# An encoder layer in one core: first-half tiles by way of DRAM, late residuals by single tiles, differences on another engine

## The chip, the cores and the metric

One core of one Trainium2 chip runs one transformer encoder layer as one program. The metric is the device time of one execution in microseconds (us). A core has TensorE (PE, matmul), VectorE (DVE), ScalarE (ACT), GpSimd (POOL) and SyncE (SP), each with its own instruction stream that runs in order. SP issues nearly all DMAs; POOL issues those that add to what lies at their destination.

## The reference

With S = 2048 tokens, D = 1024, FFN_HIDDEN = 2816, float32, and one layer, only the attention mixer is used:

```python
def rmsnorm(x, g):
    return x * lax.rsqrt(jnp.mean(x * x, axis=-1, keepdims=True) + EPS) * g

def swiglu(h, w_in, w_out):
    a, b = jnp.split(h @ w_in, 2, axis=-1)
    return (jax.nn.silu(a) * b) @ w_out

mod = silu(c) @ ada_w + ada_b
sh1, sc1, g1, sh2, sc2, g2 = split(mod, 6)
h = rmsnorm(x, mix_norm_pre) * (1 + sc1) + sh1
y = windowed_gqa_sink(h, w_qkv, w_o, sink, rel_bias)
x = x + g1 * rmsnorm(y, mix_norm_post)
h = rmsnorm(x, ffn_norm_pre) * (1 + sc2) + sh2
y = swiglu(h, w_in, w_out)
x = x + g2 * rmsnorm(y, ffn_norm_post)
```

## The kernel before

The work is kept transposed: a tile is 128 features by 512 tokens (`CH`). The tokens form four chunks c = 0 to 3, two to a half (`hf` = 0 and 1). The stages follow each other: Q, K, V and their statistics; attention with the output projections filled in (to about 820 us of the profile); the hidden products of the feed-forward (820 to 1690), half by half, each in blocks t = 0 to 21; its output products (1690 to 2125), half by half in four parts of the hidden tiles (`PARTS`); and the end of the second half. Every float32 product is made of three products of a high and a low part. `split` makes these parts: a cast on ACT (L158) and a subtraction on DVE (L159); `three` (L153 to L155) issues the matmuls.

Both feed-forward products use a scheme with seven products of half-size blocks in place of eight. `Block.__init__` loads two raw weight slabs from a pool of two buffers (`raw`, L749 and L750, names wiri and wiro), forms four sums on DVE (L754 to L758) and splits seven operands. `Block.step` runs one of the seven products into one of six PSUM buffers. `Hidden.take` combines the results: additions on DVE that read PSUM (L801 to L817), and then Silu on ACT and a product of the two halves on POOL (L827). The activations also need sums of blocks: `differences` (L526 to L533) forms four of them from a pair of hidden tiles, `give_pair` stores them to `g_d` (L782), and the output stage reads them as hb11o, ht2o and so on (L736).

The first half's residual and norm after attention are done before the hidden stage. Those of chunks 2 and 3 are done beside the hidden blocks of the first half, by the generator `late_residuals`, of which the table `LATE` says how many steps follow each block: y is read back (ly), multiplied by its norm on POOL (L863), x is added by an accumulating DMA of POOL's (L864), the result is stored (L857), squared on ACT (L859) and the squares are added on POOL (L861); then the second norm gives h2 (lh, L505), and for chunk 3 the differences. `late_ada` follows it with the last adaLN products on DVE (L901).

`Outs.take` copies the first part's seven products to z tiles (ACT, L969), a ring of 31 buffers, and adds later parts on DVE (L972); the combinations of L976 run on DVE or POOL. A finished tile is `ys[c, n]`. `square` squares it on ACT (L990) and adds it to zacc (L991). `ends` then forms the norm with `rstd_out`, and `finish` scales each tile on DVE (L1000), adds the attention's residual x1 by an accumulating DMA of POOL's (L1001) and stores it to the output by SP (L1002). For the first half this runs beside the second half's first products, a step for each turn of `interleaved`. `rstd_of` takes the mean by a matmul with ones, then Ln, Exp and Square on ACT and one Newton step on DVE (L144, L145); for that the gains are scaled by -0.5 once.

A scheduler orders each engine's instructions after the program is written. It keeps dependences and buffers, and goes by a simulated time, so a small change of the source moves many instructions.

## Time and profile before

| what | value |
|---|---|
| median of 3 runs | 2178.55 us (2174.4 to 2181.18) |
| the profiled execution | 2181.28 us, its span 2179.5 us, mean granted PE clock 0.982 |
| busy of the span | PE 2053.1 us (94%), DVE 1606.6 (74%), ACT 1069.2 (49%), POOL 870.4 (40%) |
| DMA | 392.69 MB, 180 GB/s over the span |

Busy times are of the span. A window's row gives the busy time of each engine in a stretch; "idle" is what is left of it. A wait's row names the waiting instruction, the one that released it, total time, count and longest. L12 is line 12 of the kernel before.

### The profile page before, as it was taken

Reading aid. Unit: us, or ns where it says so; the run is one execution under the profiler, and the core shown is the slowest. Engines: PE = TensorE matmul, PEld = TensorE weight load, DVE = VectorE, ACT = ScalarE, POOL = GpSimd, SP = SyncE. Lnnn points to the kernel's source line nnn. Section 1 sums busy time; section 2 is a strip of 40 time slices with the busy share of each in tenths; the row PEclk is TensorE's granted clock in tenths of the full one; section 3 lists DMA queues with packets and bytes.
Section 4 is the critical chain, followed back from the end, with each engine's and each line's share of the span. In section 5 each row is a group of like instructions: output and inputs, shape, how many; then the busy total and the mean of one; then the engine's idle time right before and its main releaser. Section 6 shows DMA issues by size and latency. Waiting matters only on the chain. (4 is left out here: it accounts for less than half of the span.)

```text
span 2179.5 us, 29140 instructions
## 1 busy us (share of the span) xinstructions
PE 2053.1 (94%) x9464; PEld 1676.2 (77%) x9464; DVE 1606.6 (74%) x2793; ACT 1069.2 (49%) x2108; POOL 870.4 (40%) x792
## 2 busy tenths in 40 slices
PE   6898999999989979999999999999999899997997
PEld 4786777778867758878878778888888688785886
DVE  7657667665675668878787788777664889997886
ACT  4536666577687745435334243333332554465422
POOL 3403343357679625475375624323212100232043
PEclk9999999999999989999999999999999999999998
DMA  8877655576667595375365663223222545349436
GB/s 283 259 253 235 188 168 185 160 276 221 228 207 265 170 352 186 122 213 174 134 178 178 236 221 135 107 83 112 99 87 83 182 140 179 99 148 268 159 97 136
DMA packets 202821, 392.69 MB, mean 180 GB/s; under 512 B 20347, under 2 KB 68524, under 8 KB 197548
## 3 DMA queue, kind: packets, MB, share of 16 engines
q1 hardware_dynamic: 194028, 378.76, 51.6%
q0 software_dynamic: 8064, 11.54, 3.3%
q8 instruction: 75, 1.23, 0.2%
q14 instruction: 78, 0.64, 0.1%
q10 hardware_dynamic: 576, 0.52, 0.1%
HBM read 266.98 MB, written 123.76 MB: 179 GB/s over the span
## 5 line engine op out<-in xcount | busy, mean ns | idle before, releaser
L442 DVE CUSTOM_DVE_ANT_0 pr<-s,bias,nsink 128x384 f32<-128x384 f32 (+1 forms) x256 | 149.0, 597 | 104.9 <-PE s L437 92.6
L153 PE MATMUL pc_i<-ht,ws_i 128*128 128x512 f32 x528 | 206.3, 391 | 4.0 <-DVE u_i L801 3.3
L155 PE MATMUL pc_i<-ht,ws_i 128*128 128x512 f32 x528 | 205.7, 390 | 0.0
L154 PE MATMUL pc_i<-ht,ws_i 128*128 128x512 f32 x528 | 205.5, 389 | 0.0
L827 POOL TENSOR_TENSOR p_i<-p_i,u_i 128x512 f32<-128x512 f32 x44 | 75.3, 1713 | 317.7 <-ACT wa_i L158 150.1
L444 ACT ACTIVATE pr<-pr,nm 128x385 f32<-128x385 f32 (+1 forms) x256 | 154.0, 605 | 70.8 <-DVE nm L442 65.7
L450 POOL TENSOR_SCALAR pr<-pr,rs 128x384 f32<-128x384 f32 (+1 forms) x256 | 147.2, 600 | 91.5 <-DVE rs L448 91.1
L976 POOL TENSOR_TENSOR z<-z,z 128x512 f32<-128x512 f32 x32 | 53.8, 1698 | 298.0 <-DVE z L972 267.6
L437 PE MATMUL s<-k,q 128*128 128x384 f32 (+1 forms) x512 | 136.8, 361 | 16.7 <-DVE nm L442 9.9
L159 DVE TENSOR_TENSOR wa_i<-wiri,wa_i 128x512 fp32r<-128x512 f32 x126 | 115.7, 918 | 48.6 <-ACT wa_i L158 48.2
L153 PE MATMUL pc_i<-hb,wa_i 128*128 128x512 f32 x352 | 140.1, 398 | 9.2 <-DVE u_i L801 6.9
L159 DVE TENSOR_TENSOR plo<-t,phi 128x512 fp32r<-128x512 f32 x184 | 121.8, 685 | 26.1 <-ACT phi L158 25.0
L155 PE MATMUL pc_i<-hb,wa_i 128*128 128x512 f32 x352 | 137.5, 391 | 0.0
L154 PE MATMUL pc_i<-hb,wa_i 128*128 128x512 f32 x352 | 137.5, 391 | 0.0
L158 ACT CAST wa_i<-wiri 128x512 fp32r<-128x512 f32 x126 | 78.3, 622 | 96.1 <-PE pc_i L155 94.6
L460 PE MATMUL t<-ident,pr 128*128 128x128 f32 x736 | 116.8, 276 | 4.5 <-POOL pr L450 3.7
L153 PEld LDWEIGHTS pc_i<-ht,ws_i 128*128 128x128 f32 x528 | 99.1, 188 | 27.0 <-DVE u_i L801 5.0
L437 PEld LDWEIGHTS s<-k,q 128*128 128x128 f32 x512 | 86.0, 193 | 41.6 <-DVE nm L442 25.0
L153 PE MATMUL py<-ol,wo 128*128 128x512 f32 x256 | 103.5, 408 | 15.2 <-ACT ol L158 7.2
L154 PEld LDWEIGHTS pc_i<-ht,ws_i 128*128 128x128 f32 x528 | 99.3, 188 | 20.5
L155 PEld LDWEIGHTS pc_i<-ht,ws_i 128*128 128x128 f32 x528 | 99.1, 188 | 20.7
L158 ACT CAST phi<-t 128x512 fp32r<-128x512 f32 x184 | 101.5, 588 | 26.1 <-PE t L460 21.1
(311 smaller groups left out, 6220.7 us busy)
## 6 DMA issues: line engine op xcount, KB each, us to landing
wiri<-w_in SPq DMA_DIRECT2D x84, 512.0 KB, 4.5
ada<-ada_w SPq DMA_DIRECT2D x40, 512.0 KB, 5.4
wiro<-w_out SPq DMA_DIRECT2D x44, 384.0 KB, 3.8
q_d<-e SPq DMA_DIRECT2D x64, 256.0 KB, 4.2
q<-q_d SPq DMA_DIRECT2D x16, 1024.0 KB, 6.2
wo<-wo_d SPq DMA_DIRECT2D x16, 1024.0 KB, 5.9
g_d_b<-p_i SPq DMA_DIRECT2D x44, 256.0 KB, 2.0
g_d_t<-p_i SPq DMA_DIRECT2D x40, 256.0 KB, 2.4
```

The lines of the kernel that those rows point to most:

```text
L153: pe.matmul(ps, w[0], h[0], start=first, stop=False)
L154: pe.matmul(ps, w[0], h[1], start=False, stop=False)
L155: pe.matmul(ps, w[1], h[0], start=False, stop=last)
L158: act.copy(hi, src)
L159: return eng.tensor_tensor(lo, src, f(hi), ALU.subtract).ins
L437: m = pe.matmul(ps[:, :n], q[:, h, jb * P:(jb + 1) * P], kk[:, i, (jb + j0) * P:(jb + j1) * P], start=i == 0, stop=i == 1)
L442: red = dve.tensor_tensor_reduce(pr[:, h, :n], ps[:, :n], bias[g][:, h, j0 * P:j1 * P], -1.0, nsink[:, hh:hh + 1], ALU.add, ALU.min, nm[:, ...
L444: act.activation(pr[:, h, :n + 1], pr[:, h, :n + 1], AF.Exp, bias=nm[:, h:h + 1], scale=-1.0, accum_out=rs[:, h:h + 1])
L450: pool.tensor_scalar(pr[:, h, :n], pr[:, h, :n], rs[:, h:h + 1], 1.0, ALU.mult, ALU.mult)
L460: pe.transpose(pt[:, h * P:(h + 1) * P], pr[:, h, jj * P:(jj + 1) * P], ident)
L827: pool.tensor_tensor(sa, sa, b, ALU.mult)
L976: (pool if (i, x) in ((2, 2), (4, 4), (5, 5), (6, 6)) else dve).tensor_tensor(sums[hf, n2, x], sums[hf, n2, x], sums[hf, n2, y], ALU.add)
```

## The change

Five edits, in the order of the program.

1. `rstd_of` takes three operations on DVE by default, and two on DVE with one more on ACT where `order` is given; the gains are no longer scaled.
2. `differences` for a pair of hidden tiles, and for the late residual, runs on DVE instead of POOL.
3. The late residual is a generator for each chunk, tile by tile, two steps to a block of the first half; its multiplications and its additions of squares are on DVE. It has 5 buffers of tag l instead of 6, and 3 of r instead of 2.
4. The pool of raw weights is opened ahead of the pools of split weights, in both stages.
5. Squares of the first half's finished tiles are added by accumulating DMAs of POOL's. Each tile is stored to `z_d`, and read back as zx into the buffers of the squares (4) when its residual is due. `interleaved` takes a step of `ends` for each block instead of for each pair, after 14 empty steps.

```diff
-LATE = 2 * (0,) + 6 * (1, 1, 2)
...
+    z_d = [dram.tile([P, KT, CH], F32, name=f"z_d{c}") for c in range(CPH)]
...
-        order(dve.scalar_tensor_tensor(t, ps, EPS, t, ALU.add, ALU.mult))
-        order(dve.scalar_tensor_tensor(r, t, -3.0, r, ALU.add, ALU.mult))
+        if order is None:
+            dve.scalar_tensor_tensor(t, ps, EPS, t, ALU.add, ALU.mult)
+            dve.tensor_scalar(t, t, -0.5, 1.5, ALU.mult, ALU.add)
+            dve.tensor_tensor(r, r, t, ALU.mult)
+        else:
+            act.activation(r, r, AF.Copy, scale=-0.5)
+            order(dve.scalar_tensor_tensor(t, ps, EPS, t, ALU.add, ALU.mult))
+            order(dve.scalar_tensor_tensor(r, t, -3.0, r, ALU.add, ALU.mult))
...
-        pool.tensor_scalar(gains, gains, -0.5, 1.0, ALU.mult, ALU.mult)
...
+    rw = open_pool(early, "rw", 2)
     wl = open_pool(early, "wl")
-    rw = open_pool(early, "rw", 2)
...
-            differences(b["b11"], b["b12"], b["b21"], b["b22"], give, (pool, pool))
+            differences(b["b11"], b["b12"], b["b21"], b["b22"], give, (dve, dve))
...
-            next(end, None)
+                next(end, None)
...
+    def late_residual(c):
...
+        for k in range(KT + 1):
+            if k < KT:
+                dve.tensor_tensor(y[k], y[k], r, ALU.mult)
+                pool.dma_start(y[k], a["xT"][c, :, k, :], accum_op=ALU.add)
+            if k < KT - 1:
+                y.append(asked(f"ly{c}_{k + 1}", y_d[c - CPH][:, k + 1, :]))
+            if k:
+                sp.dma_start(x1_d[c][:, k - 1, :], y[k - 1])
+                sq = late(f"xsq{c}_{k}") if k > 1 else acc
+                act.activation(sq, y[k - 1], AF.Square)
+                if k > 1:
+                    dve.tensor_tensor(acc, acc, sq, ALU.add)
+            yield
...
-            for _ in range(1 if hf else LATE[t]):
-                next(late, None)
+                if i in (3, 6)[hf:]:
+                    next(late, None)
...
+    rw = open_pool(ctx, "rw2", 2)
     wl, wr = open_pool(ctx, "wl2"), open_pool(ctx, "wr2", side="right")
-    rw = open_pool(ctx, "rw2", 2)
...
-            eng.tensor_tensor(accs[c][:, cols], accs[c][:, cols], sq, ALU.add)
+            pool.dma_start(accs[c][:, cols], sq, accum_op=ALU.add)
...
-                square(c, k, eng=dve)
+                square(c, k)
+                sp.dma_start(z_d[c][:, k, :], ys[c, k])
...
+        def asked(c, k):
+            z = yp.tile([P, CH], F32, tag="sq", name=f"zx{c}_{k}", bufs=4)
+            sp.dma_start(z, z_d[c][:, k, :])
+            return z
+
+        for _ in range(14):
+            yield
         for c in range(CPH):
-            yield
             r = rstd_out(c)
+            z = asked(c, 0)
             yield
             for k in range(KT):
-                finish(c, k, r)
-                if k % 2:
+                last, z = z, asked(c, k + 1) if k + 1 < KT else None
+                for _ in range(2):
                     yield
+                finish(c, k, r, last)
+                yield
```

DVE at the boundary from hidden to output products, before. u2_i1_19 is the last combination of hidden block 19 of the second half; wiro0_0_0 is the first raw weight of the output products, s1 and s2 its sums, wa11, ws2 and wa12 its split parts; hb11o and hb21o are activations:

```order
L817 TENSOR_TENSOR u2_i1_19_15378<-pc6_i1_19_15441,u2_i1_19_15378 128x512
L159 TENSOR_TENSOR hb21o0_0_2_15528<-hb21o0_0_2_15528 128x512
L159 TENSOR_TENSOR wa11_o0_0_0_15540<-wiro0_0_0_15532,wa11_o0_0_0_15540 128x384
L754 TENSOR_TENSOR s1_o0_0_0_15535<-wiro0_0_0_15532 128x384
L755 TENSOR_TENSOR s2_o0_0_0_15536<-s1_o0_0_0_15535,wiro0_0_0_15532 128x384
L756 TENSOR_TENSOR wiro0_0_0_15532<-wiro0_0_0_15532 128x3x128
L758 TENSOR_TENSOR wiro0_0_0_15532<-wiro0_0_0_15532,s2_o0_0_0_15536 128x3x128
L159 TENSOR_TENSOR ws2_o0_0_0_15544<-s2_o0_0_0_15536,ws2_o0_0_0_15544 128x384
L159 TENSOR_TENSOR wa12_o0_0_0_15547<-wiro0_0_0_15532,wa12_o0_0_0_15547 128x384
L159 TENSOR_TENSOR wa11_o0_0_1_15570<-wiro0_0_1_15562,wa11_o0_0_1_15570 128x384
```

The same place now; lines are 5 to 6 higher than before (L165 is the split, L812 to L816 are additions that read PSUM):

```order
L812 TENSOR_TENSOR u3_i1_19_15421<-pc3_i1_19_15408,u2_i1_19_15391 128x512
L165 TENSOR_TENSOR wa11_o0_0_0_15553<-wiro0_0_0_15545,wa11_o0_0_0_15553 128x384
L165 TENSOR_TENSOR ws2_o0_0_0_15557<-s2_o0_0_0_15549,ws2_o0_0_0_15557 128x384
L763 TENSOR_TENSOR wiro0_0_0_15545<-wiro0_0_0_15545,s2_o0_0_0_15549 128x3x128
L165 TENSOR_TENSOR wa12_o0_0_0_15560<-wiro0_0_0_15545,wa12_o0_0_0_15560 128x384
L165 TENSOR_TENSOR wa11_o0_0_1_15583<-wiro0_0_1_15575,wa11_o0_0_1_15583 128x384
L165 TENSOR_TENSOR hb11o0_0_0_15509<-hb11o0_0_0_15509 128x512
L814 TENSOR_TENSOR u2_i1_19_15391<-pc4_i1_19_15423,u2_i1_19_15391 128x512
```

The first weight's sum s1 stands 15 rows ahead of block 19's addition of product 3 (L812 now, L807 before) and stood 15 rows behind it; the weight's first splits now stand ahead of those of the activations.

The late residual of chunk 2 on POOL beside hidden block 4, before (lacc2 the sum of squares, ly2 the tiles, p1 and u2 the hidden block's own):

```order
L861 TENSOR_TENSOR lacc2_9394<-lacc2_9394,xsq2_1_9547 128x512
L827 TENSOR_TENSOR p1_i0_4_9442<-p1_i0_4_9442,u3_i0_4_9487 128x512
L861 TENSOR_TENSOR lacc2_9394<-lacc2_9394,xsq2_2_9707 128x512
L863 TENSOR_TENSOR ly2_4_9554<-ly2_4_9554,lr2_9235 128x512
L863 TENSOR_TENSOR ly2_5_9556<-ly2_5_9556,lr2_9235 128x512
L861 TENSOR_TENSOR lacc2_9394<-lacc2_9394,xsq2_3_9711 128x512
L827 TENSOR_TENSOR u2_i0_4_9457<-u2_i0_4_9457,b1_i0_4_9503 128x512
L864 DMA ly2_4_9554<-xT 128x512
```

The same residual now, on DVE beside block 3; wiri0_5 is the next weight:

```order
L866 TENSOR_TENSOR ly2_3_9509<-ly2_3_9509,lr2_9197 128x512
L165 TENSOR_TENSOR wa11_i0_5_9578<-wiri0_5_9570,wa11_i0_5_9578 128x512
L806 TENSOR_TENSOR u2_i0_3_9317<-pc1_i0_3_9304,p1_i0_3_9302 128x512
L165 TENSOR_TENSOR ws2_i0_5_9582<-s2_i0_5_9574,ws2_i0_5_9582 128x512
L763 TENSOR_TENSOR wiri0_5_9570<-wiri0_5_9570,s2_i0_5_9574 128x4x128
L808 TENSOR_TENSOR p1_i0_3_9302<-pc2_i0_3_9319,p1_i0_3_9302 128x512
L165 TENSOR_TENSOR wa12_i0_5_9585<-wiri0_5_9570,wa12_i0_5_9585 128x512
L875 TENSOR_TENSOR lacc2_9256<-lacc2_9256,xsq2_2_9512 128x512
L812 TENSOR_TENSOR u3_i0_3_9347<-pc3_i0_3_9334,u2_i0_3_9317 128x512
L165 TENSOR_TENSOR ws3_i0_5_9588<-wiri0_5_9570,ws3_i0_5_9588 128x512
L875 TENSOR_TENSOR lacc2_9256<-lacc2_9256,xsq2_3_9567 128x512
L866 TENSOR_TENSOR ly2_4_9564<-ly2_4_9564,lr2_9197 128x512
```

Its multiplications and additions stand between the additions that read products pc1 to pc3 from PSUM. The add of a tile's square stands some ten rows behind the tile's multiplication (ly2_1, two rows ahead of the first row shown, belongs to xsq2_2).

SP at the end of the first half, before (z0 its tiles, ht2o1_1 and hb21o1_1 the operands of the second half's second part):

```order
L736 DMA ht2o1_1_0_17927<-g_d1_0_t2_217 128x512
L736 DMA ht2o1_1_1_17931<-g_d1_1_t2_225 128x512
L1002 DMA out<-z0_0_2_15698 128x512
L736 DMA ht2o1_1_2_17935<-g_d1_2_t2_233 128x512
L1002 DMA out<-z0_0_5_15770 128x512
L736 DMA hb21o1_1_0_17969<-g_d1_0_b21_218 128x512
L1002 DMA out<-z0_1_2_15710 128x512
L736 DMA hb21o1_1_1_17973<-g_d1_1_b21_226 128x512
L736 DMA hb21o1_1_2_17977<-g_d1_2_b21_234 128x512
```

SP there now:

```order
L1020 DMA z_d1_355<-z0_3_4_16047 128x512
L1020 DMA z_d0_354<-z0_3_5_16083 128x512
L1020 DMA z_d1_355<-z0_2_6_16107 128x512
L1020 DMA z_d1_355<-z0_3_6_16119 128x512
L1027 DMA zx0_0_17969<-z_d0_354 128x512
L1027 DMA zx0_1_17983<-z_d0_354 128x512
L1027 DMA zx0_2_18048<-z_d0_354 128x512
L1027 DMA zx0_3_18101<-z_d0_354 128x512
L754 DMA wiro1_1_0_18154<-w_out 128x768
L755 DMA wiro1_1_0_18154<-w_out 128x768
L754 DMA wiro1_1_1_18273<-w_out 128x768
```

The stores to the output that stood among these operands are gone from there. The tiles' stores to z_d and the first four reads of zx stand ahead of the second part's weights (wiro1_1); the output's stores follow among later operands.

More of the change, by code (lines that the diff above doesn't have):

```diff
@@ new lines, in late_residual, with late, asked @@
+    def late_residual(c):
+        def late(name):
+            return temp(name, "l", 5)
+        def asked(name, src):
+            t = late(name)
+            sp.dma_start(t, src)
+            return t
+        r = temp(f"lr{c}", "r", 3)
+        acc = asked(f"lacco{c}", acc_d[c - CPH])
+        yield
+        rstd_of(temp, psF, "mm", acc, f"lo{c}", r, direct=True, order=lambda m: m)
+        acc = temp(f"lacc{c}", "r", 3)
+        y = [asked(f"ly{c}_0", y_d[c - CPH][:, 0, :])]
+        yield
[12 more added lines that the diff above has]
+            yield
+        r = temp(f"lr2{c}", "r", 3)
+        rstd_of(temp, psF, "mm", acc, f"l{c}", r, direct=True, order=lambda m: m)
+        x1 = [asked(f"lh{c}_0", x1_d[c][:, 0, :])]
+        first = {}
+        yield
+        for k in range(KT):
+            make_h2(x1[k], c, k, r)
+            if c == NCH - 1 and k % 2 == 0:
+                first = [asked(f"ld{k + e}", h2_d[c - 1][:, k + e, :]) for e in range(2)]
+            if k < KT - 1:
+                x1.append(asked(f"lh{c}_{k + 1}", x1_d[c][:, k + 1, :]))
+            if c == NCH - 1 and k % 2:
+                differences(first[0], x1[k - 1], first[1], x1[k],
+                            lambda n, t: sp.dma_start(hd_d[1][k // 2][n], t) if n[0] == "t" else None, (dve, dve))
+            yield
@@ L891, in late_ada @@
+    def late_residuals():
+        chunks = [late_residual(c) for c in range(CPH, NCH)]
+        for s in range(20 + 12):
+            for i, g in enumerate(chunks):
+                if s >= 12 * i:
+                    next(g, None)
+            yield
+        assert all(next(g, None) is None for g in chunks)
     def late_ada():
```

63 lines of the change are left out of this document (10 added, 53 removed).

## The prediction

> **What bounds the kernel now.** I read the stretches of the span first, to see where TensorE (PE) is not busy, then its waits in those stretches, then the chain of waits behind the longest of them. The windows (columns: stretch, its length, busy time and instructions of PE, PE's weight loads, VectorE (DVE), ScalarE (ACT) and GpSimd (POOL), then granted PE clock, DMA share, GB/s):
>
> ```profile
> 0.00:820.00 820.00, 746.94 (x3616) 599.81 (x3617) 538.10 (x1202) 517.55 (x1119) 399.00 (x471) 0.98 0.69 231
> 820.00:1690.00 870.00, 854.46 (x3733) 700.51 (x3732) 652.13 (x848) 322.75 (x535) 374.83 (x245) 1.00 0.44 146
> 1690.00:1720.00 30.00, 22.55 (x80) 16.82 (x79) 29.11 (x44) 18.35 (x37) 7.63 (x5) 0.83 0.62 224
> 1720.00:1890.00 170.00, 170.00 (x751) 140.70 (x750) 147.77 (x274) 86.34 (x176) 6.92 (x5) 1.00 0.44 141
> 1890.00:1960.00 70.00, 67.24 (x288) 54.79 (x287) 66.63 (x106) 37.92 (x73) 24.67 (x14) 0.98 0.39 131
> 1960.00:2005.00 45.00, 33.11 (x124) 24.37 (x123) 34.18 (x60) 25.51 (x48) 11.77 (x14) 0.92 1.08 297
> 2005.00:2125.00 120.00, 120.00 (x578) 101.37 (x577) 105.20 (x178) 45.78 (x88) 24.50 (x16) 1.00 0.40 130
> ```
>
> From 820 us on PE is the bound; what can be won there are its gaps. They lie in three places: 870 - 854.46 = 15.5 us spread over the hidden blocks, 30 - 22.55 = 7.5 at their end, and 2.8 + 11.9 = 14.7 around the end of the first half's output products. A gap has a second price: the clock row falls after it. (1 - clock) x length gives 5.1 us of clock lost in 1690 to 1720, 1.4 in 1890 to 1960 and 3.6 in 1960 to 2005; around the longest gap of the hidden blocks it is 1.7, from this row:
>
> ```profile
> 1122.00:1132.00 10.00, 5.26 (x18) 3.92 (x17) 9.99 (x8) 3.84 (x7) 7.49 (x8) 0.83 0.86 211
> ```
>
> What PE waited for, in the hidden blocks, at their end, and from 1890 to 2005 (total, times, longest):
>
> ```profile
> PE pc_i L153 <- DVE u_i L801: 10.2, 6, 4.7
> ```
> ```profile
> PE pc_o L155 <- DVE wa_o L159: 3.1, 1, 3.1
> PE pc_o L153 <- ACT ws_o L158: 2.6, 1, 2.6
> PE pc_o L153 <- ACT wa_o L158: 1.8, 1, 1.8
> ```
> ```profile
> PE pc_o L153 <- DVE z L972: 6.0, 2, 3.5
> PE pc_o L153 <- ACT z L969: 5.9, 5, 1.7
> PE pc_o L153 <- ACT ws_o L158: 2.8, 1, 2.8
> ```
>
> So the first place waits for DVE to free a product's PSUM buffer, the second for split weights, the third for z tiles.
>
> **First half's end (1890 to 2005).** Two queue rows (of ACT and of SP) and the chain of waits, in order of time, say why z is late:
>
> ```profile
> ACT z L969 <- DMA out<-z: 5.1, 5, 2.1
> ```
> ```profile
> SPq L1002 <- DMA z<-x_d: 13.2, 8, 3.0
> ```
> ```profile
> 1970.72 7.06 DMA z<-x_d
> 1977.80 0.34 SPq L1002
> 1978.23 7.37 DMA ht1o<-g_d_t
> 1985.65 14.22 DMA wiro<-w_out
> ...
> 2000.44 0.70 DVE z L972
> 2001.18 0.80 PE pc_o L153
> ```
>
> The ring of 31 z tiles frees a first-half tile only when its output is stored, and these stores stand in SP's queue ahead of the second half's operands and weights, each behind its accumulating DMA. The change stores each z to DRAM as soon as it is complete: 16 SP DMAs that need no statistic, so the ring is free some 50 us earlier; the residual then works on a copy, zx (16 reads on SP, 16 scalings on DVE, 16 accumulates on POOL, 16 stores). SP still waits in order: the stores of zx still stand among the second half's operands, and the first four reads of zx stand ahead of the second part's weights and wait for a buffer of the squares. These come free by the new accumulates of the squares on POOL, which replace 14 DVE adds and form two chains of 7, because each adds into the same tile. One link is an issue plus a landing, 1.2 + 7.1 = 8.3 us by the rows here and below, so the last four links of a chain take 33 us. The reads then come at about 1926, when the first part of the second half is still running; the cover is some 10 us by my estimate, or 2.5 us more for each of the four links. All this place costs now is 14.7 + 5.0 = 19.7 us. I take back two thirds, **-13**; the bounds are -19.7 and, if SP's waits simply move to the zx reads and stores, 0.
>
> The Trainium skill, page DMA: Bandwidth & Descriptors, in its table of failure cases, says that an accumulating DMA reads its destination and writes it later and nothing holds the bytes in between, so another accumulate must wait for the earlier one's semaphore. This speaks against moving these adds: they must be serial. No run here shows an unordered pair; the order of this kernel keeps them serial, and the 33 us above stand without the rule.
>
> **Boundary (1690 to 1720).** DVE is busy 29.11 of 30 us; among its rows are the four additions that prepare the first w_out tile, the last two here:
>
> ```profile
> 1702.73 0.55 DVE L756 TENSOR_TENSOR wiro<-wiro 128x384 f32<-128x384 f32 x1
> 1703.31 0.56 DVE L758 TENSOR_TENSOR wiro<-wiro,s_o 128x384 f32<-128x384 f32 x1
> ```
>
> With the raw-weight pool opened first, the weights of the first two output blocks are asked for ahead of the last stores of the hidden blocks, and four preparations and four splits (8 x 0.55 = 4.4 us at least) leave the full stretch for one where DVE is busy 652 of 870. The three stalls of 7.5 us go down to about 2.5, and their clock of 5.1 to 2: **-8**; the bounds are -12.5 (all) and -3 (the four additions of the last pair's differences, now on DVE, take 4 x 0.68 back and the clock still falls).
>
> **Differences and late residuals (820 to 1690).** On POOL they cost, and to DVE they also did:
>
> ```profile
> L527 POOL TENSOR_TENSOR u_i<-u_i,u_i 128x512 f32<-128x512 f32 x20 | 29.0, 1452 | 1.4
> L526 POOL TENSOR_TENSOR p_i<-u_i,p_i 128x512 f32<-128x512 f32 x20 | 28.6, 1432 | 4.8 <-DMA g_d_b<-p_i 3.4
> L531 POOL TENSOR_TENSOR u_i<-u_i,p_i 128x512 f32<-128x512 f32 x20 | 28.0, 1398 | 63.0 <-DMA g_d_b<-u_i 63.0
> ```
> ```profile
> L756 DVE TENSOR_TENSOR wiri<-wiri 128x512 f32<-128x512 f32 x41 | 64.1, 1564 | 0.0
> L758 DVE TENSOR_TENSOR wiri<-wiri,s_i 128x512 f32<-128x512 f32 x42 | 52.8, 1256 | 1.3
> ```
> ```profile
> 1117.99 8.87 DVE L758 TENSOR_TENSOR wiri<-wiri,s_i 128x512 f32<-128x512 f32 x1
> 1126.79 0.68 DVE L801 TENSOR_TENSOR u_i<-pc_i,p_i 128x512 f32<-128x512 f32 x1
> ```
>
> A DVE addition of two SBUF tiles takes 0.68 us when POOL leaves it alone and up to 8.87 beside POOL's; the longest PE gap stands right behind that one. 80 + 16 differences, 16 multiplications and 14 additions move: 126 x 0.68 = 86 us more on DVE. On POOL 96 x 1.43 + 30 x 1.74 = 189 us go, half of its 374.83. The excess of the two groups above is 41 x 0.88 + 42 x 0.58 = 60 us; with as much again in the many splits of weights I take 120 and half of it gone, 60. DVE stands at 652 + 86 - 60 = 678 of 870: not the bound on average. But it is by place. A hidden block has 84 matmuls, 854.46 / 3733 x 84 = 19.2 us, and DVE's order has some 20 operations in most, 30 and 27 in the two blocks of a late chunk, and 34, 34, 33 and 30 in blocks 14 to 17, where the late adaLN products meet the late differences: 131 x 0.69 = 90 us against 77. I take 6 us of PE wait for the missing 13, since earlier blocks have 5 us to spare each. In the late chunks the new thing is a wait in order: DVE adds a square only when an accumulating DMA has landed and ACT has squared the tile, and behind that add stand the additions that free PSUM. The rows (tile ly; duration min/median/max in ns; and the landing):
>
> ```profile
> L863 POOL TENSOR_TENSOR ly<-ly,lr x16: 1522/1741/1939, 917.1 to 1120.5; 128x512 f32<-128x512 f32 x16
> L864 POOL DMA_DIRECT2D ly<-xT x16: 872/1188/1881, 925.6 to 1125.3; - x16
> L857 SPq DMA_DIRECT2D x_d<-ly x16: 319/320/372, 930.1 to 1132.2; - x16
> L859 ACT ACTIVATE xsq<-ly x14: 618/633/637, 933.5 to 1132.3; 128x512 f32<-128x512 f32 x14
> ...
> DMA to landing us min/median/max: 2.0/4.2/7.9
> ```
> ```profile
> ly<-xT POOLq DMA_DIRECT2D x16, 256.0 KB, 6.2
> ```
>
> From a multiplication to the add of its square pass 1.2 + 6.2 + 0.6 = 8.0 us; DVE has 9 to 14 rows in between, 6.2 to 9.7 us. So about half of the adds hold DVE by some 1 to 2 us: 7 us a chunk, of which the six PSUM buffers (a product every 19.2 / 7 = 2.7 us) hide half. I take 3 us of PE a chunk, 6 together, and 3 of lost clock: 15 new against 15.5 + 1.7 old, **-2**, with bounds of -17 and +14 (nothing hidden).
>
> On the time of that DMA the Trainium skill differs: page DMA: Bandwidth & Descriptors, section on the anatomy of the SWDGE path, gives 2.0 us plus the bytes over 436 KB per us, by my estimate 2.6 us for 256 KB. By it no add would wait, and the forecast would be 9 us lower. The trace has 6.2 at the median, and I keep that.
>
> **The rest.** The three-operation rstd adds one DVE operation to eight statistics of the first 820 us, and its weight loads meet the early w_in reads: **+2**, bounds -3 and +6. The 16 scalings now run behind the second half's products, where DVE is already busy 105.2 of 120; 12 of them x 0.75 is 9 us, 95%: **+2**, bounds 0 and +6. In the last 55 us a statistic gets one more ACT copy beside its DVE operation: 0.
>
> The sum is -13 - 8 - 2 + 2 + 2 = -19 on the profiled execution's 2181.3 us: 2162.3. That execution lay 2.7 us above the median of 2178.55, so the median becomes 2159.6, say **2160**.
>
> **The rivals.**
> - *Waits only change places* (17 in 100). SP's waits at the first half's end stand before zx instead of z, and the boundary gives 5: 0 - 5 - 2 + 4 = -3, so 2175. For it: DMA share is 1.08 in 1960 to 2005 and the change adds 32 transfers of 256 KB there. Against: the new stores wait for no statistic.
> - *Everything is recovered* (13 in 100): -19.7 - 12.5 - 10 + 1 = -41, so 2138. For it: the three stretches between these gaps show PE at 170 of 170 and 120 of 120.
> - *DVE waits in order in the late chunks* (28 in 100, the slower side). If the accumulate lands x us later than 6.2, each of 14 adds holds DVE by x more and PE with it once PSUM is full: 14 x. At 9.0 us that is 39, so 2199. It decides from 14 x = 25, x = 1.8, a landing of 8.0. For it: the late residual's transfers meet those of w_in, and the 8.87 us row shows PE stopped at once by one late DVE operation. Against: the longest landing of these tiles is 7.9.
>
> **How the numbers follow.** Forecast 42, recovered 13, places 17, in order 28. A measurement of this kernel can tell 0.3%, 6.5 us, from no change: 2172 to 2185. Faster takes the forecast, the recovered case and 4 of the places case (59), same takes the other 13, slower the in-order case (28). The range reaches from 2137, just below the recovered case, to 2198, where the in-order case has a landing of 8.9; about 5 in 100 lie below and 14 above.
>
> **What would show it.** Right: no wait of ACT's z copy for an output store; PE idle from 1890 to 2005 under 5 us; the boundary's stall under 4; DVE busy near 680 in the hidden blocks and L756's successor near 1.1 us; POOL near 190 there. Wrong: waits of PE for u_i above 17 us beside DVE waits for ACT's xsq; SP waiting for zx while PE waits for w_out's weights; PE gaps after 2005.

## The result: no change, and the profile after

The changed kernel takes 2177.24 us (median of 12 runs, 2173.8 to 2182.14), the kernel before 2177.66 in the same sessions (12 runs); the ratio is 0.9998, 95% interval 0.9987 to 1.001. The forecast was 2160. The profiled execution took 2177.23 us, its span is 2175.5. Its line numbers are 5 to 11 higher than before (split L164 and L165, products L159 to L161, z copies L980, z additions L983). The windows of the changed kernel, columns as before:

```profile
0.00:820.00 820.00, 742.84 (x3628) 600.36 (x3628) 545.96 (x1224) 522.68 (x1128) 400.69 (x470) 0.97 0.70 232
820.00:1690.00 870.00, 862.50 (x3766) 709.42 (x3765) 668.96 (x978) 326.49 (x544) 174.97 (x124) 0.99 0.45 150
1690.00:1720.00 30.00, 20.70 (x67) 15.97 (x66) 21.77 (x41) 15.70 (x32) 0.53 (x1) 0.77 0.34 116
1720.00:1890.00 170.00, 169.71 (x749) 140.13 (x748) 147.85 (x269) 82.53 (x170) 13.17 (x11) 1.00 0.49 156
1890.00:1960.00 70.00, 67.50 (x288) 54.74 (x287) 51.33 (x79) 37.42 (x73) 24.64 (x20) 0.98 0.78 224
1960.00:2005.00 45.00, 41.77 (x174) 33.23 (x173) 38.64 (x70) 26.41 (x55) 7.07 (x8) 0.96 0.87 257
2005.00:2125.00 120.00, 110.29 (x529) 90.36 (x528) 106.09 (x174) 41.34 (x84) 32.16 (x24) 0.99 0.54 165
```

PE's gaps have left the hidden blocks (7.5 us for 15.5) and 1890 to 2005 (5.7 for 14.7). They have grown at the boundary (9.3 for 7.5) and appeared behind 2005 (9.7 for none). PE's waits of over 1 us in the changed kernel, from 820 to 1690, from 1690 to 1720, from 1890 to 2005 and from 2005 to 2125:

```profile
PE pc_i L159 <- DVE u_i L822: 6.2, 3, 3.1
```
```profile
PE pc_o L159 <- ACT ws_o L164: 5.2, 1, 5.2
PE pc_o L159 <- ACT z L980: 4.1, 1, 4.1
```
```profile
PE pc_o L159 <- DVE z L983: 2.5, 1, 2.5
PE pc_o L159 <- ACT z L980: 2.3, 1, 2.3
```
```profile
PE pl L159 <- DVE z L983: 2.8, 2, 1.6
PE pc_o L159 <- ACT ws_o L164: 2.3, 1, 2.3
PE pc_o L159 <- DVE z L983: 2.2, 1, 2.2
PE pc_o L159 <- ACT hb22o L164: 1.7, 1, 1.7
```

Fixed windows cut the two programs at different work, so for all that follows I took the length from one matmul to another: the last attention score, the fifth and the 29th hidden block of 84 matmuls, the first output product, and the first product of each output part (H1 is the first half, H2 the second; the last column runs to the last matmul of the last part). Each is read from one profiled execution; the kernels are those of the experiments below.

| kernel | start | to block 4 | blocks 4-28 | to outputs | H1 part 1 | parts 2, 3 | part 4 | H2 part 1 | part 2 | part 3 | part 4 |
|---|---|---|---|---|---|---|---|---|---|---|---|
| before | 733.3 | 175.7 | 482.1 | 305.0 | 69.5 | 95.3 | 61.9 | 66.2 | 66.9 | 57.2 | 47.0 |
| after | 728.7 | 179.3 | 473.1 | 305.0 | 72.4 | 95.3 | 57.8 | 62.5 | 66.6 | 65.5 | 50.3 |
| e1 last pair on GpSimd | 731.4 | 179.1 | 477.0 | 305.0 | 68.1 | 95.3 | 57.8 | 62.0 | 66.8 | 65.2 | 51.1 |
| e2 no scaling | 726.6 | 181.0 | 474.0 | 305.0 | 72.3 | 95.3 | 58.2 | 76.2 | 61.8 | 57.2 | 48.0 |
| e3 stores by GpSimd | 733.6 | 179.4 | 474.1 | 305.0 | 71.9 | 95.3 | 57.4 | 62.6 | 68.0 | 66.8 | 49.7 |
| e4 before + edit 5 | 731.8 | 175.4 | 481.5 | 305.0 | 69.3 | 95.3 | 57.3 | 62.5 | 64.7 | 66.1 | 53.9 |
| e5 before + edit 4 | 730.4 | 178.8 | 480.5 | 305.0 | 68.1 | 95.3 | 63.9 | 64.7 | 67.4 | 57.2 | 47.0 |
| e6 before + edit 2 | 730.9 | 176.0 | 486.1 | 305.0 | 74.4 | 95.3 | 61.6 | 65.6 | 65.5 | 57.2 | 47.0 |
| e7 before + edit 3 | 732.7 | 176.4 | 477.7 | 305.0 | 69.3 | 95.3 | 62.2 | 65.2 | 67.1 | 57.2 | 47.0 |
| e8 early scaling | 728.7 | 181.0 | 474.8 | 305.0 | 69.6 | 95.3 | 57.2 | 61.8 | 71.8 | 58.9 | 48.9 |
| e9 pairs on GpSimd | 730.8 | 179.0 | 475.0 | 305.0 | 67.4 | 95.3 | 57.3 | 62.7 | 65.2 | 65.7 | 50.5 |
| e10 no edit 5 | 726.9 | 181.8 | 474.6 | 305.0 | 67.6 | 95.3 | 61.6 | 65.9 | 68.1 | 57.2 | 47.0 |
| e11 scaling on GpSimd | 729.2 | 180.7 | 474.7 | 305.0 | 66.6 | 95.3 | 57.8 | 69.5 | 69.5 | 67.5 | 50.2 |
| e12 old pool order, hidden | 725.5 | 174.3 | 477.5 | 305.0 | 69.5 | 95.3 | 63.3 | 66.2 | 69.5 | 57.2 | 47.3 |

Where PE is fed without a gap a stretch repeats to 0.1 us (305.0 and 95.3 in all fourteen). The start scatters by some 8 us, also between kernels that do not differ there (726.6 to 733.6), so its 4.6 us between before and after is not read as a gain. It is more than the two spans differ by (4.0; the medians differ by 0.4, and the profiled execution of before lay 3.6 us above its median). The rest: -9.0 in the hidden blocks and -8.1 up to H2's part 3 are gained; +3.6 on the way to block 4, +2.9 at the boundary, +8.3 in H2's part 3 and +3.3 in the last part are given back. That is +1.0 in sum, which is no more than the scatter.

### The profile page after: what moved, and what is told of

Read it like the earlier page. It is cut to its first block, busy times and chain, and to the rows that moved or that the text cites. A ratio compares the mean times of both kernels' runs of the same rounds, so it can differ in the third digit from the quotient of the medians.

```text
span 2175.5 us, 29168 instructions
## 1 busy us (share of the span) xinstructions
PE 2050.4 (94%) x9464; PEld 1678.4 (77%) x9464; DVE 1612.2 (74%) x2913; ACT 1068.0 (49%) x2118; POOL 674.3 (31%) x679
## 5 line engine op out<-in xcount | busy, mean ns | idle before, releaser
L832 POOL TENSOR_TENSOR p_i<-p_i,u_i 128x512 f32<-128x512 f32 x44 | 70.9, 1613 | 501.7 <-DVE u_i L819 306.7
L159 PE MATMUL pc_i<-ht,ws_i 128*128 128x512 f32 x528 | 205.9, 390 | 0.7 <-DVE u_i L819 0.5
L161 PE MATMUL pc_i<-ht,ws_i 128*128 128x512 f32 x528 | 205.7, 390 | 0.0
L449 ACT ACTIVATE pr<-pr,nm 128x385 f32<-128x385 f32 (+1 forms) x256 | 153.8, 604 | 69.5 <-DVE nm L447 64.6
L159 PE MATMUL pc_i<-hb,wa_i 128*128 128x512 f32 x352 | 138.9, 395 | 0.6 <-DVE u_i L806 0.6
L161 PE MATMUL pc_i<-hb,wa_i 128*128 128x512 f32 x352 | 137.0, 389 | 0.0
L165 DVE TENSOR_TENSOR plo<-t,phi 128x512 fp32r<-128x512 f32 x184 | 121.6, 684 | 17.4 <-ACT phi L164 16.0
L164 ACT CAST wa_i<-wiri 128x512 fp32r<-128x512 f32 x126 | 78.2, 620 | 96.7 <-PE pc_i L161 96.7
L159 PE MATMUL py<-ol,wo 128*128 128x512 f32 x256 | 103.1, 406 | 17.1 <-ACT ol L164 9.8
L159 PEld LDWEIGHTS pc_i<-ht,ws_i 128*128 128x128 f32 x528 | 99.1, 188 | 22.4 <-DVE u_i L819 1.0
L161 PEld LDWEIGHTS pc_i<-ht,ws_i 128*128 128x128 f32 x528 | 99.1, 188 | 20.6
L164 ACT CAST phi<-t 128x512 fp32r<-128x512 f32 x184 | 100.7, 589 | 22.3 <-PE t L465 17.6
L465 PEld LDWEIGHTS t<-ident,pr 128*128 128x128 f32 x736 | 90.7, 141 | 19.4 <-POOL pr L455 5.1
```

Of the source, the lines that this page charges most:

```text
L159: pe.matmul(ps, w[0], h[0], start=first, stop=False)
L161: pe.matmul(ps, w[1], h[0], start=False, stop=last)
L164: act.copy(hi, src)
L165: return eng.tensor_tensor(lo, src, f(hi), ALU.subtract).ins
L449: act.activation(pr[:, h, :n + 1], pr[:, h, :n + 1], AF.Exp, bias=nm[:, h:h + 1], scale=-1.0, accum_out=rs[:, h:h + 1])
L465: pe.transpose(pt[:, h * P:(h + 1) * P], pr[:, h, jj * P:(jj + 1) * P], ident)
```

## The experiments

Each is set against the kernel before on the same chip; the medians are of 11 or 12 runs, of 5 for e6 and of 6 for e11 and e12. The before medians of the four sessions are 2176.6 (e1 to e4), 2176.8 (e5 to e8), 2176.2 (e9 to e11) and 2178.1 (e12).

**e1: the last pair's differences back on GpSimd.**

```diff
-            differences(..., give, (dve, dve))
+            differences(..., give, (pool, pool) if hf and j == HT // 2 - 2 else (dve, dve))
```

> The changed kernel, with the differences of the last hidden pair alone (blocks 18 and 19 of the second half) back on GpSimd. Queue theory: at the boundary SP's store of those differences waited 8.6 us for VectorE's L536, and the weight of the fourth output block behind it was asked for at 1705.96 only; with the differences on GpSimd the store goes earlier, PE's wait of 4.1 us for ACT z L980 falls under 1 us, the first output part (72.4 us from the first output product to the second part; 69.5 before) comes to 66 to 69, and the run is 4 to 7 us shorter than the changed kernel's 2177. Rival (VectorE is simply full at the boundary): four operations of 0.68 us less, 72.4 goes to about 70 and the wait of 4.1 stays, because the fourth weight still stands behind stores in SP's queue.

Measured: 2171.23 us, ratio 0.9978 (0.9966 to 0.9991); H1's part 1 68.1. First the changed kernel's SP wait at the boundary, its request of the fourth weight, and ScalarE's order there:

```profile
SPq L787 <- DVE u_i L536: 8.6, 1, 8.6
```
```profile
1705.96 0.33 SPq L754 DMA_DIRECT2D wiro<-w_out  x1
```
```profile
1707.71 0.51 ACT L164 CAST ws_o<-s_o 128x384 fp32r<-128x384 f32 x1 [5.71 <-DVE s_o L760]
1708.13 0.51 ACT L164 CAST wa_o<-wiro 128x384 fp32r<-128x384 f32 x1
1709.49 0.51 ACT L164 CAST wa_o<-wiro 128x384 fp32r<-128x384 f32 x1 [0.85 <-DMA wiro<-w_out]
1709.91 3.02 ACT L980 COPY z<-pc_o 128x512 f32<-128x512 f32 x6
```

Then e1's request of the fourth weight, ScalarE's order, and the only wait of PE from 1690 to 1720:

```profile
1713.93 0.33 SPq L754 DMA_DIRECT2D wiro<-w_out  x1
```
```profile
1710.34 0.51 ACT L164 CAST wa_o<-wiro 128x384 fp32r<-128x384 f32 x1
1710.75 1.55 ACT L980 COPY z<-pc_o 128x512 f32<-128x512 f32 x3
...
1716.30 0.52 ACT L164 CAST ws_o<-s_o 128x384 fp32r<-128x384 f32 x1
```
```profile
PE pc_o L159 <- ACT ws_o L164: 7.8, 1, 7.8
```

The run is 6 us shorter and the wait of 4.1 us is gone, as the queue theory forecast, but not by the path that it named. The store of the last differences does wait 8.6 us in SP's queue for VectorE. Yet e1, which is without that wait, asks for the fourth weight later: 21.5 us behind its first output product (at 1692.4), where the changed kernel has 20.0 (from 1686.0), because SP then waits as long for a split that frees the weight's buffer. What differs is ScalarE's order. In the changed kernel the first copies of z, which free PSUM, stand behind casts of the third and the fourth weight, and ScalarE is idle 5.71 us until VectorE has formed the third weight's sums, and 0.85 for the fourth weight to land. In e1 three copies stand ahead of these casts. The traces of e6 and e8 bear this out: there too the copies stand behind a cast that waits for such sums, and PE waits for a copy, although e8 has the differences on GpSimd. So the runs show that the differences on VectorE cost this time; that they do it through ScalarE's order is read from the traces, and no run changes that order alone.

The other wait stays and takes it over in part: 5.2 becomes 7.8. Of the 4.3 us that part 1 gains, 1.5 are idle time of PE (9.3 to 7.8). The other 2.8 are PE's slower pace after a wait: without gaps the part's matmuls take 57.2 us, and beyond that and the idle time it has 5.9 in the changed kernel and 3.1 in e1.

**e2: the first half's scaling left out.**

```diff
-        order(dve.scalar_tensor_tensor(z, z, coef[:, 3, k:k + 1], r, ALU.mult, ALU.mult))
+        if c >= CPH:
+            order(dve.scalar_tensor_tensor(z, z, coef[:, 3, k:k + 1], r, ALU.mult, ALU.mult))
```

> The changed kernel without the 16 scalings of the first half's zx tiles on VectorE (the first half's output is then x1 + z unscaled); every DMA stays. VectorE theory: the third part of the second half (from its first product to the first of the last part: 65.5 us after, 57.2 before) is long because 8 scalings and a norm stand in VectorE's queue where it is busy 30.00 of 30; without them 57 to 59, and the run is 6 to 8 us shorter. Queue theory: it is long because SP waits for zx DMAs ahead of the operands (hb11o asked for at 2017.8, DVE idle 4.2 and 3.8 us for it); without the scalings the accumulates go earlier, but SP still waits for each in order: 62 to 65 and at most 3 us shorter.

Measured: H2's part 3 is 57.2, as before, and the last part 48.0. The run is 2175.47, ratio 0.9993 (0.9982 to 1.0003), because part 1 grew to 76.2. In that part ScalarE waits 20.6 us for two weights, with copies of z behind the casts, and a weight is asked for in SP's queue behind a store of zx (L1014) that waits for its accumulate:

```profile
1948.75 4.69 DMA zx<-x_d
1953.46 0.33 SPq L1014
...
1954.84 6.70 DMA wiro<-w_out
1961.56 0.51 ACT wa_o L164
1962.08 0.49 ACT z L980
1962.61 0.64 PE pc_o L159
```

The windows of part 3, of before, after and e2:

```profile
2055.80:2113.00 57.20, 57.20 (x253) 47.33 (x252) 53.24 (x84) 17.29 (x32) 18.16 (x12) 1.00 0.38 123
```
```profile
2040.60:2106.10 65.50, 60.75 (x253) 47.89 (x252) 62.11 (x98) 20.68 (x41) 21.01 (x15) 0.97 0.62 193
```
```profile
2050.40:2107.60 57.20, 57.20 (x254) 47.35 (x253) 51.86 (x83) 17.18 (x32) 17.35 (x11) 1.00 0.37 121
```

VectorE (the third busy time) has 53.24 us of work in a part that PE does in 57.2. The change brings 14 operations and 8.9 us more: four scalings stand in the part and four right ahead of it, and the rest is work that they push over from part 2. The part takes 65.5, with VectorE busy 95% of it. That agrees with the VectorE theory. But e2 does not settle it: with part 1 13.7 us longer the residual's last store goes out at 2014.8, 36 us ahead of part 3, so that SP's waits for zx are gone from part 3 as well as the scalings.

**e3: the first half's stores issued by GpSimd.**

```diff
-        sp.dma_start(out[c, :, k, cols], z)
+        (pool if c < CPH else sp).dma_start(out[c, :, k, cols], z)
```

> The changed kernel with the first half's 16 stores to the output issued by GpSimd, behind the accumulates it issues itself, so that SP no longer waits for them. Queue theory: the third part of the second half falls from 65.5 to 58 to 60 us, the second from 66.6 to 63 or less, and the run is 5 to 9 us shorter than 2177. VectorE theory: 64 to 66 and no change beyond 2 us. GpSimd now waits about 7 us for each accumulate; if that holds up the additions of L987, PE waits appear after 2060 for z L987.

Measured: 2176.58 us, ratio 0.9999 (0.9989 to 1.0009); part 3 66.8, part 2 68.0. In the changed kernel SP's waits for these stores look like the culprit (its row from 1915 to 2060):

```profile
SPq L1013 <- DMA zx<-x_d: 39.6, 10, 9.3
```

But the run does not take the waiting out of SP's queue. In the same stretch of e3 SP now stands at the reads of zx, for a buffer that is free only when an earlier tile's store has landed, and another 13.0 us at them for accumulates:

```profile
SPq L1027 <- DMA out<-zx: 25.7, 6, 7.4
```

That is 38.7 us in place of 39.6. So e3 shows only that it does not matter which of the two instructions waits; the queue theory for part 3 stands untested.

**e4: edit 5 alone on the kernel before** (z_d and zx, squares by accumulating DMAs, a step per block).

```diff
-            eng.tensor_tensor(accs[c][:, cols], accs[c][:, cols], sq, ALU.add)
+            pool.dma_start(accs[c][:, cols], sq, accum_op=ALU.add)
...
+                sp.dma_start(z_d[c][:, k, :], ys[c, k])
```

> The kernel before with edit 5 alone: squares added by accumulating DMAs, z tiles stored to DRAM and read back as zx, steps of the residual per block. If the stage lengths of the two profiles are the work of this edit: the last part of the first half and the first two parts of the second come to 58, 62.5 and 66.6 us (61.9, 66.2 and 66.9 before), the third part to 65 (57.2) and the end to 3 more: in sum no gain, +-3 us against 2177.7. Rival: the loss at the third part comes from the other edits (weights asked for earlier, buffers in another place); then it stays near 57 and the run is 6 to 9 us shorter than before.

Measured: 2177.24 us, ratio 1.0002 (0.999 to 1.0013). The stretches are those of the changed kernel: -4.6, -3.7 and -2.2 up to part 3, then +8.9 and +6.9. So gain and loss at the end both belong to edit 5. By the runs it is worth nothing in sum; this one profile has +5.3.

**e5: edit 4 alone on the kernel before.**

```diff
+    rw = open_pool(early, "rw", 2)
     wl = open_pool(early, "wl")
-    rw = open_pool(early, "rw", 2)
```

The same is done to the output stage's pools.

> The kernel before with edit 4 alone: the pool of raw weights opened first in both stages. If the early weights are worth what was forecast (8 us), the first output part falls from 69.5 to 61 to 63 us. If what the changed kernel with GpSimd's last differences showed holds (68.1, the second weight's sums waiting in VectorE's order behind the splits of ht3o and ht1o), it is 67 to 69 and the gain is 1 to 2 us. From the last attention product to hidden block 4 it costs either nothing (175.5 as before) or the 3.6 us seen after (179.1): w_in's early reads stand ahead of the last output-projection weights. Run: -2 to +3 us against before.

Measured: 2176.54 us, ratio 1.0 (0.9989 to 1.0012). The boundary gains 1.4 us, not 8: the three waits of before (7.5) have become one of 7.9. PE is idle no less, so the gain is pace: beyond 57.2 us and the idle time the part has 3.0 us instead of 4.8. The way to block 4 takes 178.8.

**e6: edit 2 alone on the kernel before.**

```diff
-            differences(..., give, (pool, pool))
+            differences(..., give, (dve, dve))
```

> The kernel before with edit 2 alone: differences of hidden pairs on VectorE instead of GpSimd. Contention theory: blocks 4 to 28 take 482 us before and 473 after; if the differences' contention with VectorE made the waits, they fall to 474 to 477. Late theory: the longest wait (4.7 us at 1127) comes of the late residual's multiplications on GpSimd (L863), which stay: 480 to 483. At the boundary VectorE has four more operations, and SP's last stores wait for it: the first output part goes from 69.5 to 71 to 74. Run: -5 to +3 us.

Measured: 2186.14 us, ratio 1.0043 (1.0027 to 1.0059), 0.4% slower. Blocks 4 to 28 take 486.1 (+4.0), the boundary 74.4 (+4.9). PE's waits at the boundary (1695 to 1730) show the copies of z once more:

```profile
PE pc_o L153 <- ACT ws_o L158: 4.0, 1, 4.0
PE pc_o L153 <- ACT z L969: 3.6, 1, 3.6
PE pc_o L155 <- DVE wa_o L159: 3.0, 1, 3.0
```

Both theories missed the hidden blocks: beside GpSimd's late multiplications, VectorE did not take the differences without harm.

**e7: edit 3 alone on the kernel before**: `late_residual` and its two steps to a block, as in the change.

> The kernel before with edit 3 alone: late residuals tile by tile, multiplications and additions of squares on VectorE, differences of hidden pairs still on GpSimd. In-order theory (waits of VectorE for the accumulating DMAs reach PE): blocks 4 to 28 take 482 us before; they become 485 or more with PE waits for L814 and L817 in blocks 3 to 5 and 9 to 11. Contention theory: GpSimd loses 30 additions and products where it starved VectorE for 8.9 us, so they fall to 475 to 478. The boundary keeps 69.5. Run: -6 to +4 us.

Measured: 2177.47 us, ratio 1.0003 (0.9993 to 1.0012). Blocks 4 to 28 take 477.7, 4.4 us less; the contention theory holds for them (the weight addition that took 1256 ns at L758 before takes 997 on the mean), the in-order theory falls. The run's median does not show those 4.4 us, and I cannot say what else took them.

**e8: early scaling, with room for the weights' first sum.** On top of e1:

```diff
-                for _ in range(2):
-                    yield
                 finish(c, k, r, last)
...
-            s1, s2 = (rw.tile([P, m, P], F32, tag=n, name=f"{n}_{u}", bufs=1) for n in ("s1", "s2"))
+            s1, s2 = (rw.tile(..., bufs=2 if nleft == 3 and n == "s1" else 1) for n in ("s1", "s2"))
...
-                q = sums[hf, n2, i] = yp.tile(..., bufs=31)
+                q = sums[hf, n2, i] = yp.tile(..., bufs=30)
```

> A version meant to beat both: the changed kernel with the last pair's differences on GpSimd, two buffers for the weights' first sum s1 in the output stage (one z buffer fewer), and the first half's residual a tile for every step instead of every third. VectorE theory: the scalings now stand in the second part of the second half, where VectorE is busy some 25 of 30 us; the third part falls from 65.5 to 57 to 60 us, the second part stays under 68. Boundary: with the second weight's sums ahead of the splits of ht3o, the remaining wait of 7.8 us falls under 4 and the first output part from 68.1 to 62 to 65. Run: 2160 to 2166 us. Rival: VectorE lacks the time wherever the scalings stand; then the second part grows by what the third gains, and the run is no better than 2168.

Measured: 2170.94 us, ratio 0.9971 (0.996 to 0.9982), faster than before but not than e1. Part 3 falls to 58.9, and part 2 grows to 71.8: 130.7 together against e1's 132.0. So the first half's residual makes the part long in which it stands, part 2 here. The run is no better than 2168, as the rival had it, but not for the rival's reason. The window of part 2:

```profile
1973.30:2045.10 71.80, 62.25 (x255) 47.82 (x253) 54.80 (x99) 29.09 (x57) 11.38 (x13) 0.98 0.91 265
```

VectorE is idle 17 of these 71.8 us; the longest of its waits is 6.7 us in total, for reads of zx (L1011). It stands in order behind the residual's DMAs and does not lack time there. At the boundary the wait for split weights is gone, and PE waits for the z copies instead:

```profile
PE pc_o L159 <- ACT z L980: 9.9, 1, 9.9
```

**e9: all hidden pairs' differences back on GpSimd**, the rest of the change kept.

```diff
-            differences(..., give, (dve, dve))
+            differences(..., give, (pool, pool))
```

> The changed kernel with the differences of all hidden pairs back on GpSimd (those of the late residual stay on VectorE). Alone on the kernel before, edit 2 cost 9 us: 4 in the hidden blocks and 5 at the boundary. If it costs the same inside the whole change, blocks 4 to 28 fall from 473 to about 470, the first output part from 72.4 to 68, and the run comes to 2168 to 2170. If edits 2 and 3 work together (with the late multiplications gone from GpSimd the hidden blocks gain from edit 2), blocks 4 to 28 grow to 476 to 478 as in the late edit alone (477.7), only the boundary gains, and the run is 2171 to 2175, no better than with the last pair alone (2171.2).

Measured: 2172.75 us, ratio 0.9978 (0.9968 to 0.9989). The boundary falls to 67.4, and blocks 4 to 28 stay at 475.0, with 473.1 to 477.5 in the other kernels that have edits 2 and 3. Inside the change edit 2 costs nothing in the hidden blocks and 5 us at the boundary. So the cost of the hidden blocks in e6 goes with the late multiplications that are on GpSimd there.

**e10: e1 with edit 5 undone** (the first half's end as in the kernel before).

```diff
-                sp.dma_start(z_d[c][:, k, :], ys[c, k])
...
-            pool.dma_start(accs[c][:, cols], sq, accum_op=ALU.add)
+            dve.tensor_tensor(accs[c][:, cols], accs[c][:, cols], sq, ALU.add)
```

> The changed kernel with the last pair's differences on GpSimd and edit 5 undone (first half's tiles finished from the z ring, squares added on VectorE). If edit 5 is a loss in sum (8 us gained up to the second part, 11.5 lost behind it), the last part of the first half returns to 62 and the third part of the second half to 57.2, and the run is 3 to 4 us shorter than 2171.2. If edit 5 is even, the run stays within 2 us of 2171.

Measured: 2171.07 us, ratio 0.9976 (0.9965 to 0.9986), e1's time. The stretches returned as expected (61.6, 57.2, 47.0). Edit 5 is even, by this and by e4.

**e11: scaling on ScalarE and GpSimd.** On top of e1:

```diff
+        if c < CPH:
+            act.activation(z, z, AF.Copy, scale=coef[:, 3, k:k + 1])
+            pool.tensor_tensor(z, z, r, ALU.mult)
+        else:
             order(dve.scalar_tensor_tensor(z, z, coef[:, 3, k:k + 1], r, ALU.mult, ALU.mult))
```

> The changed kernel with the last pair's differences on GpSimd, and the first half's 16 scalings made by ScalarE (times the coefficient) and GpSimd (times the norm) instead of VectorE; all work is done. VectorE theory: the third part falls from 65.2 to 57 to 60 us and the end from 51 to 48, so the run is 6 to 10 us shorter than 2171.2. Rival: GpSimd's 16 products of about 1.6 us hold up VectorE's additions of two SBUF tiles by as much as the scalings took; then the third part stays at 62 or more and the run within 3 us of 2171.

Measured: 2185.55 us, ratio 1.0038 (1.0024 to 1.0052), 0.4% slower; part 3 67.5. The groups of VectorE in e11 from 1940 to 2116 and, of the changed kernel, from 1940 to 2110:

```profile
L983 DVE TENSOR_TENSOR z<-pc_o,z 128x512 f32<-128x512 f32 x52 | 35.0, 678 | 0.0
...
L165 DVE TENSOR_TENSOR ht2o<-ht2o 128x512 fp32r<-128x512 f32 x6 | 6.7, 1136 | 0.2 <-ACT ht2o L164 0.2
```
```profile
L165 DVE TENSOR_TENSOR ht2o<-ht2o 128x512 fp32r<-128x512 f32 x6 | 4.0, 684 | 0.2 <-ACT ht2o L164 0.2
```

and GpSimd's products in e11:

```profile
L1013 POOL TENSOR_TENSOR zx<-zx,nrz 128x512 f32<-128x512 f32 x16 | 24.9, 1569 | 87.7 <-DVE nrz L151 60.4 <-ACT zx L1012 27.3
```

16 operations of 0.74 us left VectorE, and its window is as full as before (62.62 us in part 3, 62.11 after): subtractions of two SBUF tiles went from 684 to 1136 ns, additions that read one operand from PSUM stayed at 678. The Trainium skill, page SBUF — State Buffer, section Who interferes with whom, says that a VectorE instruction with two SBUF inputs contends with a GpSimd instruction that reads SBUF, and one with at most one SBUF input, outside the two-port fast modes, does not. These rows agree (ht2o is the group that slowed most; ht1o, ht4o and hb11o, the same operation, kept 677 to 688 ns). The largest loss against e1 stands elsewhere: part 1 takes 69.5 us instead of 62.0. There ScalarE's copies of z stand behind the new scalings, which wait 7.9 us for reads of zx, and PE waits 4.5 us for these copies.

**e12: e10 with the old pool order in the hidden stage.**

```diff
-    rw = open_pool(early, "rw", 2)
     wl = open_pool(early, "wl")
+    rw = open_pool(early, "rw", 2)
```

> A version meant to beat the others: the changed kernel with the last pair's differences on GpSimd, edit 5 undone, and the raw weights' pool of the hidden stage again opened behind the split weights' (the output stage keeps the new order). Queue theory: the first w_in reads, asked for at 776 us ahead of the last output-projection weights in the changed kernel and at 805 before, cost the 3 to 5 us between the last attention product and hidden block 4 (175.5 before, 179 to 182 since edit 4); now 175 to 177, and the run is 3 to 4 us shorter than 2171.1. The first output part stays at 67.6 if the early w_out reads need only the second pool's place, and returns to 69.5 if they need both. Rival: the 4 us belong to the late residual's first reads or to the norm; then 179 to 182 stays.

Measured: 2169.27 us, ratio 0.9963 (0.9948 to 0.9977), the fastest kernel of the study by its median, 8.9 us under the before of its session; its interval overlaps those of e1, e8, e9 and e10. The way to block 4 falls from 181.8 (e10) to 174.3, with the first w_in read at 797.5 instead of 775.4, so the hidden stage's pool order, which puts these reads ahead of the last output-projection weights, costs those microseconds; later stretches give most of them back, and the run's median gains 1.8. The boundary returns to 69.5: the first w_out read goes out 10.0 us ahead of the first output product, as in the kernel before, and 37.7 where both pools are in the new order.

## Why the prediction was wrong

- **The sum.** By stretches the five terms came to: first half's end -8.1 for -13, boundary +2.9 for -8, hidden blocks -9.0 for -2, start +3.6 for +2, scalings +11.6 for +2. That is +1.0 for -19. The boundary and the scalings are the two steps that failed, and both lie outside the bounds given for them; the hidden blocks, 7.0 us better than forecast, hid part of it.
- **What held.** The forecast for the first half's end: z no longer waits for a store, and up to H2's part 3 the change gains 8.1 us of the 13 taken. The chain of accumulates cost PE nothing that this trace shows: they landed in 4.1 us at the median, where I had 7.1. The first four reads of zx waited 15.4 us for them in SP's queue and came at 1937, not 1926, but PE's only gap of that part had ended at 1920. Short of the 13, part 2 gained next to nothing (66.6 for 66.9).

```profile
zacc<-zsq POOLq DMA_DIRECT2D x14, 256.0 KB, 4.1
```

- **The first failed step: the 16 scalings behind the second half's products, +2.** Edit 5 costs 8.3 us in part 3 and 3.3 in the last part; without it both are as before (e10), and e4 has the loss with edit 5 alone. I added 9 us to 105.2 of 120 and read 95% as room. The stretch was too long: part 3 alone had 53.24 of 57.2. Only eight scalings, 6 us, stand in it or right ahead of it, but VectorE came to it late. Its waits in part 2, first before, then in the changed kernel:

```profile
DVE z L972 <- PE pc_o L155: 7.5, 12, 0.9
```
```profile
DVE ht1o L165 <- ACT ht1o L164: 4.4, 2, 4.1
DVE s_o L759 <- DMA wiro<-w_out: 4.2, 1, 4.2
DVE hb11o L165 <- ACT hb11o L164: 3.8, 1, 3.8
```

Before, it had caught up with PE and waited mostly for it. In the changed kernel it waits 12.4 us, for a weight and for operands that ScalarE casts, and SP stands 22.8 us of part 2 at stores that wait for accumulates into zx; then it is busy 62.11 of 65.5. Leaving that waiting out of the term, and taking a share of 120 us for room, is the step that failed. How the 11.6 us divide between VectorE's time and SP's queue stays open: e2 and e8 move both out of part 3, and e3 and e11 leave the waiting where it was.

- **The second failed step: the boundary, -8, had the wrong sign (+2.9).** Two things were missed. The last pair's differences on VectorE cost 4.3 to 5 us (e1, e6, e9); I had priced them as four operations of 0.68, and the traces show copies of z late on ScalarE in their place (e1). And moving the first weight forward is worth 1.4, not 8 (e5): the three waits merge into one of about 8 us in e1, e5, e9 and e10, and become one of 9.9 for the copies in e8.
- **The hidden blocks, -2, were under-sized (-9.0 here; 473.1 to 477.5 in the kernels with edits 2 and 3, 480.5 to 482.1 without either).** DVE was busy 669 us, forecast 678, and POOL 175. Edit 3 alone gains 4.4 us (e7), edit 2 alone loses 4.0 (e6), and with edit 3 in place edit 2 changes nothing beyond the scatter (e9): I had priced the two as one. The waits of an add for the square of its tile, on which the slower rival rested, come to 3.9 us in three places. The two additions of weights that I took for relieved went apart: L763 (L758 before) fell from 1256 to 738 ns, L761 (L756 before) stayed at 1558.

```profile
DVE lacc L875 <- ACT xsq L873: 3.9, 3, 2.0
```
```profile
L761 DVE TENSOR_TENSOR wiri<-wiri 128x512 f32<-128x512 f32 x40 | 62.3, 1558 | 0.0
...
L763 DVE TENSOR_TENSOR wiri<-wiri,s_i 128x512 f32<-128x512 f32 x40 | 29.5, 738 | 1.1
```

- **The rest, +2 for the start.** Edit 4's cost on the way to block 4 was there: 3.1 us in e5, 3.6 in the change. The norm's extra operation was not tried by itself, and its stretch scatters by some 8 us.
- **The rivals.** The result is near that of the case "waits only change places" (17 in 100), 2175, but by chance: its terms were 0, -5, -2 and +4, and the measured ones are -8.1, +2.9, -9.0 and +15.2. Of its mechanism the waiting of SP for zx is there, 39.6 us (e3); what that costs is not shown. PE gaps after 2005, which I had named as a sign of being wrong, are there too (9.7 us).
- **Still open.** How the loss of parts 3 and 4 divides, as said above. Why e2's first part grew to 76.2 is read from its trace and not tested. The 4.4 us of e7's blocks that its run does not show, too.

## What to carry to other kernels

Add moved work to the busy time of the stretch in which it lands, cut no longer than the buffers can bridge, and ask when that engine gets its operands: part 3 had 93% of 57 us taken already, and VectorE came to it late from waits for operands. Work that is moved together with its DMAs brings their waits into an in-order queue; follow that queue to the next load behind them. An engine's busy time is not the price of work moved onto it: look at what then stands behind what on the other engines, such as the copies here that free PSUM. When three waits have one cause, such as a splitting engine that is full, moving one of its jobs can merge the waits rather than remove them.

## What the runs showed of the hardware

An accumulating DMA of 256 KB landed in 4.1 us at the median where 14 of them ran (zacc), and in 5.9 to 6.1 for ly and zx in the same run (its DMA rows: count, KB, median us to landing), all above the Trainium skill's figure (DMA: Bandwidth & Descriptors, anatomy of the SWDGE path), by my estimate 2.6 us:

```profile
ly<-xT POOLq DMA_DIRECT2D x16, 256.0 KB, 5.9
...
zx<-x_d POOLq DMA_DIRECT2D x16, 256.0 KB, 6.1
```

A PE wait also slows the matmuls behind it. The first output part has 252 matmuls, which take 57.2 us when PE is fed without a gap. Beyond that and the idle time the part is 1.6 to 3.1 us longer in the kernels with a single wait of 7.8 to 9.9 us (e1, e5, e8 to e11), and 5.2 to 5.9 in those with two, of 5.2 and 4.1 to 4.3 us (the change, e2, e3). (1 - clock) x length, by which the prediction priced this, also counts the low clock of the wait itself: in e1 it gives 5.1 us for 1696 to 1726 (clock 0.83), against 3.1 by the length.
